# A projection of two gates in one pass, and a scan with its fillers in another order

## The chip, the cores and the metric

The kernel runs on one core of one Trainium2 chip. A core has TensorE (PE in the profile, with PEld for its weight loads), VectorE (DVE), ScalarE (ACT), GpSimd (POOL) and SyncE (SP, which issues nearly all DMAs here). The metric is device microseconds of one execution. Every engine works through its own list of instructions in order, and waits where the next one's inputs or its target buffer are not ready.

## The reference

One encoder layer over 1024 positions of width 1024, in float32: a normalized input goes through one projection whose columns feed four mixers, their outputs are joined, projected and added to the input; then a gated feed-forward layer follows. What matters here, cut short:

```python
proj = einsum('bsd,de->bse', rmsnorm(h), w_in)
y_a = pool_mixer(p_pool)                    # running means over 2, 4, 8, 16 positions, then a small product
y_b = p_u * mixed(layernorm(p_v))           # spatial gating: a 128x128 product along positions, gated by u
y_c = p_cb * causal_conv(p_cc * p_ch)       # short convolution, three projections of 256 columns
y_d = ssd(p_z, p_x, p_b, p_c, p_dt)         # a scan over chunks; its output is gated by silu(p_z), then normalized
h = h + concat(y_a, y_b, y_c, y_d) @ w_out
h = h + (silu(rmsnorm(h) @ w_gate) * (rmsnorm(h) @ w_up)) @ w_down
return rmsnorm(h)
```

## The kernel before

A program builds the lists of instructions; a scheduler inside it orders them by its own estimate of time, and an explicit `follow(i, j)` makes instruction i stand behind j on their engine. Nearly all large products are done in three passes (`mm3`, or the loop of `proj_T`): each operand is split into a high and a low part, and high x high, high x low and low x high are summed. An operand's split is a copy on ACT (the line of `nc.scalar.copy` in `split`) and a subtraction on DVE.

Two forms of projection come from the input x (`xh`, `xl`, eight tiles of 128 rows). `proj_T(i)` takes 128 columns of the weights and gives a result with channels on the partitions: 48 products with 512 columns each, into two banks of PSUM. `proj_N` gives 128 positions on the partitions: 24 products, here with 256 columns for z and 256 for u, into one bank. Weights for these are loaded raw into one of two buffers (`wraw`) and split into one of four pairs (`whi`, `wlo`).

The order of work: the projections of the scan's inputs (`proj_T` 0 to 5, of which 5 is the last), then z for eight blocks of 128 positions (`pn_z`, gated by ACT into `sz`, which lies in mix 4 and 5), then the scan. The scan is `ssd_block(b, prev)` for b = 0 to 7, in the profile the products `pt_x` (transposes of the inputs), `pg` (scores), `py` (the output; its second part takes the state `prev`) and `pst` (the new state). On DVE a block turns the scores into `Gm`, multiplies them into the decays `E`, and makes `xd`, `xe` and a first `y` out of `xb`, which ACT copies from `pt_x`; after `py` it adds up y and makes the next `prev`. All these small products take their PSUM from one pool of three banks (`pss`), in turn, and a bank is free again when what stands in it has been read. `ssd_end` normalizes finished blocks: a power on POOL, a scaling on DVE and the transposes `pty`.

Behind each block stands one part of the list `fill`: work that has nothing to do with the scan and keeps TensorE busy while DVE and ACT make the block's inputs. Before, that list is: the spatial gating of blocks 0 to 3 (with the four products `pm` and the projections `pn_u`), the gating of blocks 4 to 7, `pooling(0)`, `pooling(1)`, and `conv_c`, `conv_h` for t = 0, then for t = 1. `conv_h(t)` ends with two sums on DVE (the second and third tap) and then one multiplication of 128x1024 on POOL. `conv_b(0)` and `conv_b(1)` stand behind the whole scan in the code, but the scheduler put them between its last blocks. In names with numbers, pt10 is `conv_b(0)`, pt12 is `conv_h(1)` and pt13 is `conv_b(1)`.

Behind that stands the output projection (`po`), which takes the mixed tiles in the order of the list `order`, then the feed-forward layer, which is more than half of the time and which the change does not touch.

Of the kernel before, what the change touches and what calls it, by code (L numbers as in the profile page):

```python
# [46 lines left out]
def encoder_kernel(ctx, tc, xT, w_t, w_z, w_vd, w_u, pool_w, sgu_wT, par, row, w_out, w_gate, w_up, w_dp, w_dl, gfin, out):  # L47
# [94 lines left out]
    mix = [acts.tile([P, S], F32, name=f"mix{i}", tag="act") for i in range(8)]  # L142


    order = [2, 3, 0, 1, 6, 7, 4, 5]
    mh, ml = [None] * 8, [None] * 8
    h1 = [None] * 8

# [21 lines left out]
    with ExitStack() as a:  # L170
# [17 lines left out]
        def pc(c):  # L188
            return part[:, c:c + 1]
# [69 lines left out]
            o = (g % 2) * 64  # L259
            nc.sync.dma_start(out=pw[o:o + 64, g // 2, o:o + 64], in_=pool_w[g])  # L260

        def proj_T(*tiles, ws=None):

            ws = ws or [load_w(w_t[i], S, f"t{i}") for i in tiles]
            pss_ = [[psm.tile([P, HS], F32, name=f"pt{i}_{h}", tag="mm") for h in range(2)] for i in tiles]
            for k in range(NK):
                ks = slice(k * P, (k + 1) * P)
                for (hi, lo), ps in zip(ws, pss_):
                    for w1, x1, first, last in ((hi, xh, True, False), (hi, xl, False, False), (lo, xh, False, True)):
                        for h in range(2):  # L270
                            nc.tensor.matmul(ps[h], w1[:, ks], x1[k][:, h * HS:(h + 1) * HS],  # L271
                                             start=(k == 0 and first), stop=(k == NK - 1 and last))
            return pss_ if len(tiles) > 1 else pss_[0]

        def evac(ps, out):
# [124 lines left out]

        def heads(t):
            return t.rearrange("p (h c) -> p h c", h=NH)

        def ssd_block(b, prev):
            bs = slice(b * P, (b + 1) * P)
            E = sb.tile([P, NH, P], F32, name=f"E{b}", tag="E", bufs=2)
            nc.sync.dma_start(out=E, in_=acsD[b * NH:(b + 1) * NH, :].unsqueeze(0).to_broadcast([P, NH, P]))
            for h in range(NH):
                V.tensor_scalar(out=E[:, h, :], in0=E[:, h, :], scalar1=acs[:, b * NH + h:b * NH + h + 1],
                                scalar2=0.0, op0=ALU.subtract, op1=ALU.min)  # L410
            nc.scalar.activation(out=E, in_=E, func=AF.Exp)
# [12 lines left out]
            E4 = E.rearrange("p (g r) l -> p g r l", g=2)
            V.tensor_tensor(out=E4, in0=E4, in1=Gm.unsqueeze(2).to_broadcast([P, 2, 2, P]), op=ALU.mult)
            xd = sb.tile([P, 256], F32, name=f"xd{b}", tag="xd", bufs=1)
            xe = sb.tile([P, 256], F32, name=f"xe{b}", tag="xe", bufs=1)
            V.tensor_tensor(out=heads(xd), in0=heads(xb[:, 0:256]), in1=per_head(delta, b), op=ALU.mult)
            V.tensor_tensor(out=heads(xe), in0=heads(xb[:, 0:256]), in1=per_head(dte, b), op=ALU.mult)
            py = pss.tile([P, 512], F32, name=f"py{b}", tag="sm")  # L430
            for h in range(NH):
                nc.tensor.matmul(py[:, h * 64:(h + 1) * 64], E[:, h, :], xd[:, h * 64:(h + 1) * 64],
                                 start=True, stop=True)
            if prev is not None:
                for g in range(2):
                    nc.tensor.matmul(py[:, 256 + g * P:256 + (g + 1) * P], cT[g][:, bs],
                                     prev[:, g * P:(g + 1) * P], start=True, stop=True)
            y = yz[b]
            V.tensor_tensor(out=heads(y), in0=heads(xb[:, 0:256]),
                            in1=rowt[:, R_D:R_D + 4].unsqueeze(2).to_broadcast([P, NH, 64]), op=ALU.mult)  # L440
            V.tensor_tensor(out=y, in0=y, in1=py[:, 0:256], op=ALU.add)
            if prev is not None:
                yo = sb.tile([P, 256], F32, name=f"yo{b}", tag="yo", bufs=1)
                V.tensor_tensor(out=heads(yo), in0=heads(py[:, 256:512]), in1=per_head(ea, b), op=ALU.mult)
                V.tensor_tensor(out=y, in0=y, in1=yo, op=ALU.add)
            V.tensor_tensor(out=y, in0=y, in1=sz[b], op=ALU.mult)
            for g in range(2):
                jk = sb.tile([P, P], F32, name=f"jk{b}{g}", tag="jk", bufs=1)
                nc.scalar.activation(out=jk, in_=y[:, g * P:(g + 1) * P], func=AF.Square,
                                     accum_out=ss[:, 2 * b + g:2 * b + g + 1])  # L450
            if b < NB - 1:
                pst = pss.tile([P, 512], F32, name=f"pst{b}", tag="sm")
                for g in range(2):
                    nc.tensor.matmul(pst[:, g * P:(g + 1) * P], xb[:, 256 + g * P:256 + (g + 1) * P],
                                     xe[:, g * P:(g + 1) * P], start=True, stop=True)
                new = sb.tile([P, 256], F32, name=f"prev{b}", tag="prev", bufs=2)
                if prev is None:
                    V.tensor_copy(out=new, in_=pst[:, 0:256])
                else:
                    V.tensor_tensor(out=heads(new), in0=heads(prev), in1=per_head(dec, b), op=ALU.mult)  # L460
                    V.tensor_tensor(out=new, in0=new, in1=pst[:, 0:256], op=ALU.add)
                prev = new
            return prev

        def ssd_end(c0, n):
# [4 lines left out]
            for b0 in range(c0, c0 + n, 2):  # L470
# [13 lines left out]
        def mix_v():
            for h in range(NH):
                pm = pss.tile([P, 512], F32, name=f"pm{h}", tag="sm")
                v = vnt[:, :, h * 64:(h + 1) * 64]
                nc.tensor.matmul(pm, wTs[:, h, :], v, start=True, stop=True)
                nc.scalar.activation(out=v, in_=pm.rearrange("p (b c) -> p b c", b=NB), func=AF.Identity,
                                     bias=pc(C_SGUB + h))  # L490


        def gating(wu, b0):
            pt = pss.tile([P, 512], F32, name=f"ptb{b0}", tag="sm")
            for b in (b0, b0 + 1):
                ps = proj_N(wu, 256, b, "u")
                mb = vn[b]
                V.scalar_tensor_tensor(out=mb, in0=ps[:, :256], scalar=rn[:, b:b + 1], in1=mb,
                                       op0=ALU.mult, op1=ALU.mult)
                for g in range(2):  # L500
                    o = g * 256 + (b - b0) * P
                    nc.tensor.transpose(pt[:, o:o + P], mb[:, g * P:(g + 1) * P], ident)
            for g in range(2):
                nc.scalar.copy(out=mix[2 + g][:, b0 * P:(b0 + 2) * P], in_=pt[:, g * 256:(g + 1) * 256])


        def pooling(t):
# [40 lines left out]
            causal_conv(ch, 3, C_SCW + 3 * t, cc)  # L548
            nc.gpsimd.tensor_tensor(out=cc, in0=cc, in1=rB, op=ALU.mult)

        def conv_b(t):
            ps = proj_T(10 + 3 * t)
            for h in range(2):
                hs = slice(h * HS, (h + 1) * HS)
                V.tensor_tensor(out=mix[4 + t][:, hs], in0=ps[h], in1=gate_c[t][:, hs], op=ALU.mult)

        wu = nat_weights(w_u, 256, "u")
        fill = [lambda: (mix_v(), gating(wu, 0), gating(wu, 2)), lambda: (gating(wu, 4), gating(wu, 6)),
                lambda: pooling(0), lambda: pooling(1), lambda: conv_c(0), lambda: conv_h(0),
                lambda: conv_c(1), lambda: conv_h(1)]  # L560
        prev = None
        for b in range(NB):
            prev = ssd_block(b, prev)
# [519 lines left out]
```

## Time and profile before

| | us |
|---|---|
| three runs, median (lowest, highest) | 1011.45 (1010.33, 1013.96) |
| the profiled execution | 1012.61 |
| its span, first to last instruction | 1010.9 |
| PE busy | 999.5 (99%) |
| DVE busy | 814.4 (81%) |
| ACT busy | 402.4 (40%) |
| POOL busy | 297.8 (29%) |

The profiled execution is 1.7 us longer than its span, and 1.16 us above the median. A product's record on PE begins when it is issued, and lasts until its last result is out; the next is issued long before that. So the time that a product costs TensorE is the distance from its start to the start of the next one, not its own length. A plain float32 product takes two passes of this kind, so one instruction can have two records.

### The profile page before, as it was taken

To read this page: it belongs to the slowest core of one execution; us is meant where nothing else is said; L and a number is where in the kernel's file an instruction comes from. 1 tells how busy PE (TensorE), PEld (TensorE's weight loads), DVE (VectorE), ACT (ScalarE), POOL (GpSimd) and SP (SyncE) were. 2 spreads that over 40 slices of the span, in tenths; PEclk is the share of its full clock that TensorE was granted. 3 is DMA by queue.
4 is the path that set the end of the run, shared out by engine and by line. 5 is a ranking of instruction groups with operands and counts; after the bars stand their busy time and mean duration, and the time that the engine had idled before them with its cause. 6 is when DMAs were issued, how large, how long until landed. Compare 5 with 4: busy or idle time off the path is not lost.

```text
span 1010.9 us, 13188 instructions
## 1 busy us (share of the span) xinstructions
PE 999.5 (99%) x4816; PEld 840.1 (83%) x4816; DVE 814.4 (81%) x1293; ACT 402.4 (40%) x736; POOL 297.8 (29%) x329
## 2 busy tenths in 40 slices
PE   9999999999999999999999999999999999999996
PEld 8988998888887878888888888888888888888885
DVE  7498336786742689989899989989898999989867
ACT  8156322132531245434343343434343343334363
POOL 0034000011011131245434434544434434444302
PEclk9999999999999999999999999999999999999999
DMA  7311112101630201122111112111111111122204
GB/s 276 105 63 64 44 42 74 52 32 54 211 101 11 74 11 42 53 63 62 59 46 63 44 53 59 57 62 63 53 46 59 53 53 53 63 63 63 64 1 167
DMA packets 29681, 67.60 MB, mean 67 GB/s; under 512 B 3720, under 2 KB 4016, under 8 KB 29616
## 3 DMA queue, kind: packets, MB, share of 16 engines
q1 hardware_dynamic: 29184, 66.44, 19.9%
q8 instruction: 38, 0.62, 0.3%
q10 hardware_dynamic: 432, 0.31, 0.1%
q14 instruction: 27, 0.22, 0.1%
HBM read 62.53 MB, written 4.21 MB: 66 GB/s over the span
## 4 chain that ended last, share of the span: by engine, by line
PE 99%; DVE 1%; issue 0%; ACT 0%; POOLq 0%; POOL 0%; ACTq 0%
PE pt L271 15%; PE po L85 3%; PE po L87 3%; PE po L86 3%; PE p L85 1%; PE p L86 1%; PE p L87 1%; PE pn_v L86 1%; PE pn_z L87 1%; PE pn_z L86 1%; PE pn_z L85 1%; PE pn_u L86 1%; PE pn_v L87 1%; PE pn_u L85 1%; PE pn_u L87 1%; PE pn_v L85 1%
## 5 line engine op out<-in xcount | busy, mean ns | idle before, releaser
L815 POOL TENSOR_TENSOR rs<-rd 128x128 f32<-128x128 f32 x40 | 25.6, 641 | 187.3 <-DMA rd<-in_w_dp 80.5
L271 PE MATMUL pt<-x_lo,wh_t 128*128 128x512 f32 x224 | 70.3, 393 | 0.0
L271 PE MATMUL pt<-x_hi,wh_t 128*128 128x512 f32 x224 | 70.1, 394 | 0.0
L271 PE MATMUL pt<-x_hi,wl_t 128*128 128x512 f32 x224 | 69.6, 391 | 0.0
L940 ACT ACTIVATE g<-g 128x512 f32<-128x512 f32 x40 | 25.3, 633 | 71.1 <-DVE g L744 71.1
L92 ACT CAST dh<-rs 128x256 fp32r<-128x256 f32 (+1 forms) x80 | 28.1, 351 | 57.9 <-POOL rs L713 2.0
L93 DVE TENSOR_TENSOR dl<-rs,dh 128x256 fp32r<-128x256 f32 (+1 forms) x80 | 48.2, 603 | 1.5 <-ACT dh L92 1.5
L271 PEld LDWEIGHTS pt<-x_hi,wl_t 128*128 128x128 f32 x224 | 42.0, 188 | 8.7
L271 PEld LDWEIGHTS pt<-x_lo,wh_t 128*128 128x128 f32 x224 | 41.8, 188 | 8.5 <-issue 0.2
L271 PEld LDWEIGHTS pt<-x_hi,wh_t 128*128 128x128 f32 x224 | 41.7, 188 | 8.5 <-issue 0.2
L944 POOL TENSOR_TENSOR g<-g,u 128x512 f32<-128x512 f32 x20 | 34.1, 1703 | 36.4 <-DVE u L744 36.4
L85 PE MATMUL po<-mix_hi,oh 128*128 128x512 f32 x112 | 44.5, 398 | 0.0
L93 DVE TENSOR_TENSOR dl<-rd,dh 128x256 fp32r<-128x256 f32 x80 | 42.9, 537 | 1.8 <-ACT dh L92 1.8
L87 PE MATMUL po<-mix_hi,ol 128*128 128x512 f32 x112 | 44.2, 395 | 0.0
L86 PE MATMUL po<-mix_lo,oh 128*128 128x512 f32 x112 | 44.1, 394 | 0.0
L92 ACT CAST dh<-rd 128x256 fp32r<-128x256 f32 x80 | 32.2, 406 | 23.7 <-PE pd92A L86 1.6
L166 DVE TENSOR_TENSOR h<-po,h 128x512 f32<-128x512 f32 x16 | 11.0, 688 | 33.3 <-PE po L87 33.3
L752 POOL TENSOR_TENSOR s1u<-ru,ru 128x512 f32<-128x512 f32 x10 | 18.2, 1817 | 62.8 <-DMA ru<-in_w_up 51.3
L93 DVE TENSOR_TENSOR wl_t<-wr_t,wh_t 128x1024 fp32r<-128x1024 f32 (+2 forms) x16 | 17.4, 1087 | 22.0 <-ACT wh_t L92 22.0
L752 POOL TENSOR_TENSOR s1g<-rg,rg 128x512 f32<-128x512 f32 x10 | 12.9, 1293 | 59.9 <-DVE wg_2l L93 27.6
L612 POOL TENSOR_TENSOR qa_h<-qa_h,q 128x512 f32<-128x512 f32 x6 | 8.3, 1375 | 65.5 <-ACT q L611 65.5
L713 POOL TENSOR_TENSOR rd<-rd 128x128 f32<-128x128 f32 x40 | 26.6, 666 | 0.0
(3153 smaller groups left out, 3393.2 us busy)
## 6 DMA issues: line engine op xcount, KB each, us to landing
rd<-in_w_dp SPq DMA_DIRECT2D x40, 256.0 KB, 2.6
rg<-in_w_gate SPq DMA_DIRECT2D x40, 256.0 KB, 2.7
ru<-in_w_up SPq DMA_DIRECT2D x40, 256.0 KB, 2.8
wr_t<-in_w_t SPq DMA_DIRECT2D x12, 512.0 KB, 3.3
or<-in_w_out SPq DMA_DIRECT2D x8, 512.0 KB, 4.1
h<-in_xT SPq DMA_DIRECT2D x8, 512.0 KB, 5.0
mix<-in_xT SPq DMA_DIRECT2D x7, 512.0 KB, 7.7
out<-hn SPq DMA_DIRECT2D x7, 512.0 KB, 2.6
```

Of the source, the lines that this page charges most:

```text
L85: nc.tensor.matmul(ps, whi, xhi, start=start, stop=False, skip_group_check=skip)
L86: nc.tensor.matmul(ps, whi, xlo, start=False, stop=False, skip_group_check=skip)
L87: nc.tensor.matmul(ps, wlo, xhi, start=False, stop=stop, skip_group_check=skip)
L92: a = nc.scalar.copy(out=hi, in_=src)
L93: b = (eng or V).tensor_tensor(out=lo, in0=src, in1=hi.bitcast(F32), op=ALU.subtract)
L166: return V.tensor_tensor(out=h1[d][:, hs], in0=ps, in1=h1[d][:, hs], op=ALU.add)
L271: nc.tensor.matmul(ps[h], w1[:, ks], x1[k][:, h * HS:(h + 1) * HS], start=(k == 0 and first), stop=(k == NK - 1 and last))
L713: eng.tensor_tensor(out=out, in0=a_, in1=b_, op=ALU.subtract)
L752: G.tensor_tensor(out=s1, in0=a21, in1=a22, op=ALU.add)
L815: G.tensor_tensor(out=s1, in0=a21, in1=a22, op=ALU.add)
L940: nc.scalar.activation(out=t, in_=t, func=AF.Silu)
L944: (V if i in (1, 2) else nc.gpsimd).tensor_tensor(out=g[i], in0=g[i], in1=t, op=ALU.mult)
```

## The change

z and u are projected together: the 256 columns of either stand side by side in a tile of weights (four tiles of two rows of x each, filled by eight DMAs in place of four), so a block has 24 products with 512 columns, whose result is read by ACT (z) and by DVE (u, gated in place). The four products `pm` now stand ahead of this. The first filler, `gated`, only transposes the gated blocks. The list of fillers is now `gated`, `pooling(0)`, `pooling(1)`, `conv_c(0)`, `conv_c(1)`, `conv_h(0)`, `conv_h(1)`, `conv_b(0)`; and `conv_b(1)` stands behind the scan, its first product ordered behind the last product of the last `py`. In `order`, mix 4 comes earlier, since `conv_b(0)` now ends earlier.

```diff
-    order = [2, 3, 0, 1, 6, 7, 4, 5]
+    order = [2, 3, 0, 1, 4, 6, 7, 5]
...
-        wz = nat_weights(w_z, 256, "z")
+        for h in range(NH):
+            pm = pss.tile([P, 512], F32, name=f"pm{h}", tag="sm")
+            v = vnt[:, :, h * 64:(h + 1) * 64]
+            nc.tensor.matmul(pm, wTs[:, h, :], v, start=True, stop=True)
...
+        wzu = []
+        for j in range(4):
+            raw, hi, lo = w_tiles(S, f"zu{j}")
+            for i, w in enumerate((w_z, w_u)):
+                nc.sync.dma_start(out=raw.rearrange("p (k c) -> p k c", k=2)[:, :, i * 256:(i + 1) * 256],
+                                  in_=w[:, 2 * j:2 * j + 2, :])
+            split(raw, hi, lo)
+            wzu.append((hi, lo))
...
         for b in range(NB):
-            ps = proj_N(wz, 256, b, "z")
-            nc.scalar.activation(out=sz[b], in_=ps[:, :256], func=AF.Silu, scale=rn[:, b:b + 1])
+            ps = psm.tile([P, HS], F32, name=f"pn_zu{b}", tag="mm")
+            bs = slice(b * P, (b + 1) * P)
+            for k in range(NK):
+                hi, lo = (w_[:, k % 2 * HS:(k % 2 + 1) * HS] for w_ in wzu[k // 2])
+                mm3(ps, xh[k][:, bs], xl[k][:, bs], hi, lo, k == 0, k == NK - 1)
+            nc.scalar.activation(out=sz[b], in_=ps[:, 0:256], func=AF.Silu, scale=rn[:, b:b + 1])
+            V.scalar_tensor_tensor(out=vn[b], in0=ps[:, 256:512], scalar=rn[:, b:b + 1], in1=vn[b],
+                                   op0=ALU.mult, op1=ALU.mult)
...
-        def conv_b(t):
-            ps = proj_T(10 + 3 * t)
+        def conv_b(t, after=None):
+            ps = proj_T(10 + 3 * t, after=after)
...
-        wu = nat_weights(w_u, 256, "u")
-        fill = [lambda: (mix_v(), gating(wu, 0), gating(wu, 2)), lambda: (gating(wu, 4), gating(wu, 6)),
-                lambda: pooling(0), lambda: pooling(1), lambda: conv_c(0), lambda: conv_h(0),
-                lambda: conv_c(1), lambda: conv_h(1)]
+        fill = [gated, lambda: pooling(0), lambda: pooling(1), lambda: conv_c(0), lambda: conv_c(1),
+                lambda: conv_h(0), lambda: conv_h(1), lambda: conv_b(0)]
...
-        conv_b(0)
-        conv_b(1)
+        conv_b(1, last_py[-1])
```

How the lists of instructions look is shown at three places. TensorE, where the last scan input (pt5) ends and the projection of z begins. Before:

```order
L271 MATMUL pt5_0_887<-x_hi7_157,wl_t5_883 128x512
L271 MATMUL pt5_1_888<-x_hi7_157,wl_t5_883 128x512
L85 MATMUL pn_z0_984<-wh_z0_973,x_hi0_143 128x256
L86 MATMUL pn_z0_984<-wl_z0_974,x_hi0_143 128x256
L87 MATMUL pn_z0_984<-wh_z0_973,x_lo0_144 128x256
```

And now:

```order
L271 MATMUL pt5_0_887<-x_hi7_157,wl_t5_883 128x512
L271 MATMUL pt5_1_888<-x_hi7_157,wl_t5_883 128x512
L394 MATMUL pm0_972<-vnt_132,wTs_233 128x512
L394 MATMUL pm1_975<-vnt_132,wTs_233 128x512
L394 MATMUL pm2_978<-vnt_132,wTs_233 128x512
L85 MATMUL pn_zu0_1012<-wh_zu0_985,x_hi0_143 128x512
L86 MATMUL pn_zu0_1012<-wl_zu0_986,x_hi0_143 128x512
L87 MATMUL pn_zu0_1012<-wh_zu0_985,x_lo0_144 128x512
```

Three of the four `pm` came forward from the scan (the fourth stands inside the first block of z and u), and a pair of products with 256 columns became one with 512. TensorE at the last block of the scan, from the end of `conv_b(0)` (pt10) on. Before (29 products of pt13 stand between `pg7` and `py7`; "..." leaves out 27 of them):

```order
L271 MATMUL pt13_0_2338<-x_lo0_144,wh_t13_2333 128x512
L414 MATMUL pt_x7_2161<-ident_70,mix6_86 128x128
...
L420 MATMUL pg7_2168<-xbc4_879,xbc2_745 128x128
L420 MATMUL pg7_2168<-xbc5_946,xbc3_812 128x128
L271 MATMUL pt13_1_2339<-x_lo0_144,wh_t13_2333 128x512
...
L271 MATMUL pt13_1_2339<-x_hi5_153,wh_t13_2333 128x512
L432 MATMUL py7_2178<-xd7_2174,E7_2154 128x64 x4
```

And now:

```order
L271 MATMUL pt10_1_2071<-x_hi7_157,wl_t10_2066 128x512
L458 MATMUL py6_1921<-xd6_1917,E6_1897 128x64 x4
L462 MATMUL py6_1921<-prev5_1829,xbc4_879 128x128
L462 MATMUL py6_1921<-prev5_1829,xbc5_946 128x128
L481 MATMUL pst6_1938<-xe6_1918,xb6_1909 128x128 x2
L505 MATMUL pty4_2012<-ident_70,yzt_133 128x128 x4
L440 MATMUL pt_x7_2030<-ident_70,mix6_86 128x128
...
L446 MATMUL pg7_2037<-xbc5_946,xbc3_812 128x128
L458 MATMUL py7_2047<-xd7_2043,E7_2023 128x64 x4
L462 MATMUL py7_2047<-prev6_1941,xbc4_879 128x128
L462 MATMUL py7_2047<-prev6_1941,xbc5_946 128x128
L271 MATMUL pt13_0_2142<-x_hi0_143,wh_t13_2137 128x512
```

Nothing stands between `pg7` and `py7` any more, and all of pt13 comes behind `py7`. DVE around the scores of block 6, with the two sums of `conv_h(1)` (SCALAR_TENSOR_TENSOR on cc1). Before, the block's last inputs came first, and the sums behind them:

```order
L422 TENSOR_TENSOR Gm6_2051<-pg6_2048,tri_134 128x256
L278 TENSOR_TENSOR ch1_2195<-pt12_0_2203,rB_131 128x512
L278 TENSOR_TENSOR ch1_2195<-pt12_1_2204,rB_131 128x512
L425 TENSOR_TENSOR E6_2034<-E6_2034,Gm6_2051 128x512
L93 TENSOR_TENSOR wl_o1_2458<-wr_o1_2456,wh_o1_2457 128x1024
L547 TENSOR_TENSOR ch1_2195<-ch1_2195,cc1_2081 128x1024
L283 SCALAR_TENSOR_TENSOR cc1_2081<-ch1_2195,part_110,cc1_2081 128x1024 x2
```

And now:

```order
L468 TENSOR_TENSOR yzt_133<-yzt_133,py5_1809 128x256
L471 TENSOR_TENSOR yo5_1818<-py5_1809,ea_658 128x256
L488 TENSOR_TENSOR prev5_1829<-prev5_1829,pst5_1826 128x256
L286 SCALAR_TENSOR_TENSOR cc1_1701<-ch1_1944,part_110,cc1_1701 128x1024
L454 TENSOR_TENSOR xd6_1917<-xb6_1909,delta_635 128x256
L455 TENSOR_TENSOR xe6_1918<-xb6_1909,dte_661 128x256
...
L435 TENSOR_SCALAR E7_2023<-E7_2023,acs_657 128x128 x4
L473 TENSOR_TENSOR yzt_133<-yzt_133,mix5_85 128x256
L448 TENSOR_TENSOR Gm6_1914<-pg6_1911,tri_134 128x256
L451 TENSOR_TENSOR E6_1897<-E6_1897,Gm6_1914 128x512
```

The chain of `conv_h(1)` now runs ahead of block 6's inputs; its second sum, which sets off the multiplication on POOL, stands just ahead of `xd6`.

## Rows read from the trace of the kernel before

**Rows 1.** The page's chain that ended last: shares of the span by engine
```profile
PE 99%; DVE 1%; issue 0%; ACT 0%; POOLq 0%; POOL 0%; ACTq 0%
```

**Rows 2.** Windows: stretch, length, busy time of each engine, PE clock, DMA
```profile
121.90:250.00 128.10, 128.10 (x740) 110.44 (x739) 85.11 (x171) 33.27 (x72) 7.70 (x6) 1.00 0.17 54
...
328.00:330.00 2.00, 2.00 (x7) 1.52 (x6) 2.00 (x5) 1.76 (x3) 0.00 (x0) 0.50 0.00 0
...
366.00:370.00 4.00, 2.74 (x10) 1.34 (x9) 3.14 (x6) 0.30 (x1) 1.68 (x4) 1.00 0.23 66
```

**Rows 3.** Timeline of ACT: reading of two blocks of z in turn: start, length, instruction
```profile
110.55 0.47 ACT L392 ACTIVATE mix<-pn_z,rs_y_x 128x256 f32<-128x256 f32 x1 [2.41 <-PE pn_z L87]
113.43 0.47 ACT L392 ACTIVATE mix<-pn_z,rs_y_x 128x256 f32<-128x256 f32 x1 [2.41 <-PE pn_z L87]
```

**Rows 4.** Timeline of PE in the output projection
```profile
315.62 0.39 PE L85 MATMUL po<-mix_hi,oh 128*128 128x512 f32 x1
...
317.44 0.39 PE L87 MATMUL po<-mix_hi,ol 128*128 128x512 f32 x1
```

**Rows 5.** Timeline of PE: blocks 6 and 7 of the scan
```profile
243.07 1.00 PE L432 MATMUL py<-xd,E 128*128 128x64 f32 x8
...
244.41 0.61 PE L454 MATMUL pst<-xe,xb 128*128 128x128 f32 x4
244.85 0.60 PE L478 MATMUL pty<-ident,yzt 128*128 128x128 f32 x4
...
250.34 0.27 PE L414 MATMUL pt_x<-ident,mix 128*128 128x128 f32 x1
...
250.77 0.61 PE L420 MATMUL pg<-xbc,xbc 128*128 128x128 f32 x4
...
257.82 1.00 PE L432 MATMUL py<-xd,E 128*128 128x64 f32 x8
```

**Rows 6.** Timeline of DVE, 230 to 253 us
```profile
230.65 0.42 DVE L444 TENSOR_TENSOR yo<-py,ea 128x256 f32<-128x256 f32 x1
...
231.31 0.42 DVE L445 TENSOR_TENSOR yzt<-yzt,yo 128x256 f32<-128x256 f32 x1
...
234.79 0.47 DVE L409 TENSOR_SCALAR E<-E,acs 128x128 f32<-128x128 f32 x2
...
237.59 1.28 DVE L278 TENSOR_TENSOR ch<-pt,rB 128x512 f32<-128x512 f32 x2
238.78 0.68 DVE L425 TENSOR_TENSOR E<-E,Gm 128x512 f32<-128x512 f32 x1
239.38 1.22 DVE L93 TENSOR_TENSOR wl_o<-wr_o,wh_o 128x1024 fp32r<-128x1024 f32 x1
...
243.01 2.60 DVE L283 SCALAR_TENSOR_TENSOR cc<-ch,part,cc 128x1024 f32<-128x1024 f32 x2 [1.28 <-ACT cc L281]
...
246.53 1.85 DVE L445 TENSOR_TENSOR yzt<-yzt,yo 128x256 f32<-128x256 f32 x1
...
251.42 0.42 DVE L422 TENSOR_TENSOR Gm<-pg,tri 128x256 f32<-128x256 f32 x1 [0.51 <-PE pg L420]
...
252.77 0.68 DVE L425 TENSOR_TENSOR E<-E,Gm 128x512 f32<-128x512 f32 x1
```

**Rows 7.** Timeline of POOL: the multiplication that ends conv_h(1)
```profile
245.69 2.40 POOL L549 TENSOR_TENSOR cc<-cc,rB 128x1024 f32<-128x1024 f32 x1 [9.27 <-DVE cc L283]
```

**Rows 8.** Timeline of ACT, 245 to 252 us
```profile
245.49 0.84 ACT L480 ACTIVATE mix<-pty,part 128x256 f32<-128x256 f32 x2 [2.51 <-PE pty L478]
...
250.97 0.59 ACT L417 COPY xb<-pt_x 128x512 f32<-128x512 f32 x1 [1.21 <-PE pt_x L415]
```

**Rows 9.** Timeline of PE where it waits in the second half of the output projection
```profile
325.59 1.12 PE L139 MATMUL ps_rows_h<-rx_h,ones 4*128 4x512 f32 x2 [1.26 <-DVE rx_h L132]
...
328.26 0.63 PE L85 MATMUL po<-mix_hi,oh 128*128 128x512 f32 x1
...
331.25 0.45 PE L86 MATMUL po<-mix_lo,oh 128*128 128x512 f32 x1
```

More of the change, by code (lines that the diff above doesn't have):

```diff
@@ L260, in encoder_kernel, with proj_T @@
             nc.sync.dma_start(out=pw[o:o + 64, g // 2, o:o + 64], in_=pool_w[g])
-        def proj_T(*tiles, ws=None):
+        def proj_T(*tiles, ws=None, after=None):
             ws = ws or [load_w(w_t[i], S, f"t{i}") for i in tiles]
@@ L270, in proj_T @@
                         for h in range(2):
-                            nc.tensor.matmul(ps[h], w1[:, ks], x1[k][:, h * HS:(h + 1) * HS],
-                                             start=(k == 0 and first), stop=(k == NK - 1 and last))
+                            i = nc.tensor.matmul(ps[h], w1[:, ks], x1[k][:, h * HS:(h + 1) * HS],
+                                                 start=(k == 0 and first), stop=(k == NK - 1 and last))
+                            if after is not None:
+                                follow(i, after)
+                                after = None
             return pss_ if len(tiles) > 1 else pss_[0]
@@ L385, in encoder_kernel @@
             nc.gpsimd.tensor_tensor(out=v, in0=v, in1=rowt[:, R_LB:R_LB + 256], op=ALU.add)
-        wz = nat_weights(w_z, 256, "z")
+        for h in range(NH):
+            pm = pss.tile([P, 512], F32, name=f"pm{h}", tag="sm")
+            v = vnt[:, :, h * 64:(h + 1) * 64]
+            nc.tensor.matmul(pm, wTs[:, h, :], v, start=True, stop=True)
+            nc.scalar.activation(out=v, in_=pm.rearrange("p (b c) -> p b c", b=NB), func=AF.Identity,
+                                 bias=pc(C_SGUB + h))
+        wzu = []
[6 more added lines that the diff above has]
+            wzu.append((hi, lo))
         sz = [mix[4 + b // 4][:, (b % 4) * 256:(b % 4 + 1) * 256] for b in range(NB)]
         for b in range(NB):
-            ps = proj_N(wz, 256, b, "z")
-            nc.scalar.activation(out=sz[b], in_=ps[:, :256], func=AF.Silu, scale=rn[:, b:b + 1])
+            ps = psm.tile([P, HS], F32, name=f"pn_zu{b}", tag="mm")
[6 more added lines that the diff above has]
+                                   op0=ALU.mult, op1=ALU.mult)
         ss = sb.tile([P, NB * 2], F32, name="ss")
@@ L402, in heads @@
             return t.rearrange("p (h c) -> p h c", h=NH)
+        last_py = []
         def ssd_block(b, prev):
@@ L435, in ssd_block @@
                 for g in range(2):
-                    nc.tensor.matmul(py[:, 256 + g * P:256 + (g + 1) * P], cT[g][:, bs],
-                                     prev[:, g * P:(g + 1) * P], start=True, stop=True)
+                    i = nc.tensor.matmul(py[:, 256 + g * P:256 + (g + 1) * P], cT[g][:, bs],
+                                         prev[:, g * P:(g + 1) * P], start=True, stop=True)
+                last_py.append(i)
             y = yz[b]
@@ L481, in ssd_end, with gated @@
                                   mul=pc(C_NG + g))
[L484 to L499, printed above, removed]
+        def gated():
+            for b0 in range(0, NB, 2):
+                pt = pss.tile([P, 512], F32, name=f"ptb{b0}", tag="sm")
+                for b in (b0, b0 + 1):
+                    for g in range(2):
+                        o = g * 256 + (b - b0) * P
+                        nc.tensor.transpose(pt[:, o:o + P], vn[b][:, g * P:(g + 1) * P], ident)
                 for g in range(2):
[L501 to L504, printed above, removed]
+                    nc.scalar.copy(out=mix[2 + g][:, b0 * P:(b0 + 2) * P], in_=pt[:, g * 256:(g + 1) * 256])
         def pooling(t):
```

## The prediction

> **What bounds the kernel.** The chain that ended last comes first: 99% of it is PE [rows 1]. Then the windows: the whole scan is one stretch in which PE is busy for 128.10 of 128.10 us, at a granted clock of 1.00, so 2.4 GHz [rows 2]. So nothing that DVE, ACT, POOL or a DMA does in the scan costs anything now. The change can gain only by giving PE less to do, and it loses wherever PE must wait. Third, the timelines give each step's price and, on the other engines, how much room each has before PE would wait. Last, the places where PE does wait already: in the output projection it stands for 1.26 us behind DVE [rows 9], and 2.4 us later the clock reads 0.50, which is 1.2 GHz [rows 2].
>
> **Term 1, the merged projection: −2.5 us.** ACT reads one finished block of z every 113.43 − 110.55 = 2.88 us, and PE does nothing else there [rows 3]: 24 products with 256 columns, 0.120 us each. A product with 512 columns takes (317.44 − 315.62) / 8 = 0.2275 us [rows 4]. Two narrow ones cost 0.240, so a merged pair saves 0.0125 us. There are 8 blocks of 24 such pairs (z and u had 192 products each): 192 × 0.0125 = 2.4 us; with the rounding of the rows 2.3 to 2.6, and I take 2.5. The four `pm` and the transposes of the gated blocks are moved, not added. The new weights' eight DMAs stand where four did, and their splits are as many columns as before; PE reaches them only after pt5, and no wait follows by my estimate. The new DVE reading of u costs what it cost in the scan, and frees it there.
>
> Saying it as a fixed cost: 256 columns at 2.4 GHz are 106.7 ns and 512 are 213.3, so each product leaves some 13 to 14 ns over [rows 3, 4]. The Trainium skill ("TensorE: Matmul & The Clock Gate", Back-to-back issue gap) gives a warm product N / 2.4 GHz plus some 2.5 ns. By that the merge would save 192 × 2.5 ns = 0.5 us and the sum below would be 2.0 us longer; the rows of this kernel say 13, in both widths, and I go by them.
>
> **Term 2, a wait before py6: +2.0 us.** In the old order E6 stood ahead of the sums of `conv_h(1)` on DVE; now the whole chain from pt12's bank to the second sum stands ahead of it (the third place of the change), with `conv_b(0)` alone, pt10, as PE's cover. I count both engines from the end of pt12.
>
> PE: 48 products of pt10 are 48 × 0.2275 = 10.92; among them py5 at 244.41 − 243.07 = 1.34, pst5 at 244.85 − 244.41 = 0.44, pt_x6 at 250.77 − 250.34 = 0.43, and pg6 about as long as pst [rows 5]. PE is ready for py6 at 13.6.
>
> DVE, if it begins at e: from reading the bank to the first sum takes 243.01 − 237.59 = 5.42, less 0.60 for the E that stood between (239.38 − 238.78): 4.82. The two sums take 2.60 together, and three small steps on py5 and pst5 stand between them; small steps follow each other at (231.31 − 230.65) / 2 = 0.33 us [rows 6]. So POOL can start its multiplication at e + 4.82 + 2.60 + 1.0 = e + 8.4. It takes 2.40 [rows 7], and here is the disputed step. In before, y += yo began 0.84 us after it, and was 1.85 us long where the same instruction elsewhere took 0.42: it ended at 248.38, just behind POOL's end at 248.09 [rows 6, 7]. The steps ahead of it that read PSUM kept their 0.42 and 0.41 [rows 6]. I read this as: a DVE operation with both operands in SBUF that starts during POOL's multiplication waits for its end. Now xd6 slips in ahead, and xe6, with both operands in SBUF, is held to about e + 11.1. Behind it stand y, y += yo, the next prev, four steps of E7 (0.40 for two [rows 6]), y × z, Gm6 and E6: 5 × 0.33 + 0.8 + 0.68 = 3.1. E6 is ready at e + 14.2.
>
> How late is e? The same count for `conv_h(0)`, one filler earlier: py4 comes 22 products (5.0) after the end of pt9 and lasts 1.34, y and yo of block 4 take DVE to about 7.1, the first sum, two small steps, E6's four and the second sum to 11.1, POOL to 13.5, the held step to 13.85, and Gm5, E5, xd5, xe5, y to 15.8. PE ends pt12 at 10.92 + 1.34 + 0.44 for pst4, 2 × 0.44 for two groups of transposes, 0.43 and 0.44: 14.45. So e is about 1.4, and the wait 14.2 + 1.4 − 13.6 = 2.0 us. Bounds: without any hold by POOL e is 0 and E6 comes at 8.4 + 2 × 0.33 + 3.1 = 12.2, no wait; with the later hold alone, 0.6; with both and a late DMA of decays, 2.6.
>
> **Term 3, a wait before py7: +3.0 us.** Before, 29 products of pt13, 6.6 us, stood between pg7 and py7, and hid DVE's work on the scores. Now nothing stands there. Count from the start of py6. py6 and pst6 end at 1.78, then comes pty4. pt_x7 needs the bank of py6, which yo6 reads last; DVE first reads pt10's two banks (1.28, as for pt12 [rows 6]) and scales four tiles for pty4 (0.8, as E7's four), so yo6 ends near 2.9. pt_x7 starts then, and pg7 ends at 2.9 + 0.43 + 0.44 = 3.75 [rows 5]. Then DVE: from the start of Gm to the end of E took 252.77 + 0.68 − 251.42 = 2.03 us [rows 6], with xd, xe and y between, and these five stand there in the same order now. Gm begins 0.2 after pg (251.42 against 250.77 + 0.44 [rows 5, 6]), so E is ready at 6.0. ACT's xb (0.59, behind 0.84 for two copies of pty [rows 8]) ends near 4.1, in time for xd. PE has 3.1 us of work in these 6.0 (1.34, three times 0.44, 0.43): it waits 2.9, I take 3.0 with the start of py7. The lower bound is DVE's five steps alone, 2.03 + 0.2 + 0.1 = 2.3, since nothing can be put between; the upper one 3.6, if pty4's scaling is late. Behind py7 stands pt13, which loses nothing else: pty6 waits behind 33 of its products, and the output projection takes mix 5 last, three products per tile and 24 per block, so that DVE has over 4 us for its two splits.
>
> **Term 4, the clock: +1.6 us.** After the first wait of 1.26 us PE ran seven products in 331.25 − 328.26 = 2.99 us, 0.427 each in place of 0.2275 [rows 9]: 1.4 us lost, and 1.6 with the edges of the stretch. The second wait, as long (2.74 busy of 4.00), was followed by none: 1.00 throughout [rows 2]. So a wait of 1.3 us brings a low stretch in one of two cases. The two new ones together idle PE for 5 us within some 10, so I take one such stretch, with none (0) and two (3.2) as bounds.
>
> **Edits at nothing.** The new order of `conv_c` and pooling: PE has the same products, and DVE, busy for 85.11 of the scan's 128.10 us [rows 2], keeps by the same count some 4 us ahead of PE in each earlier block. `order` with mix 4 earlier only follows conv_b(0). If this cover is gone, the price is that of a wait like term 2's.
>
> **Sum.** 1012.61 − 2.5 + 2.0 + 3.0 + 1.6 = 1016.7 for an execution like the profiled one; that one was 1.16 above the median, so the median comes at **1015.6**, 0.4% over 1011.45. From no change this measurement can tell about 0.3%, 3.0 us.
>
> **Rivals.**
> - All four terms as above, 0.53. Its own range is 1013.8 to 1016.8: terms 2 and 3 together go from 3.2 to 6.2 in place of 5.0.
> - *Not slower:* POOL's multiplication doesn't hold xe6 (or the DVE chain runs early enough), so E6 is ready before PE. Place: DVE, from xd6 to E6. For it: the hold is read from one row. Against it: 1.85 against 0.42 [rows 6]. Term 2 goes: 1013.6, within 0.3%. It decides as soon as py6 waits less than about 0.9 us, since 1014.5 is the limit. 0.20.
> - The clock stays at 2.4 GHz after the waits, as after the second old one [rows 2]: 1014.0. 0.10.
> - The change does only what the merge does, and the waits are hidden: 1011.45 − 2.5 = 1008.9; against it stands term 3's lower bound of 2.3. It is faster by over 0.3% if the merge, and DVE's freed time in the scan, give 0.6 more than the rows say. 0.08, half of it faster.
> - Two low stretches, or the decays of block 7 late: 1.6 more, 1017.2. 0.07.
> - The merge saves 0.5, not 2.5: 1017.6. Only the rows' 13 ns per product speak against it. The page named above would have it so. 0.02.
>
> Within 0.3% (1008.4 to 1014.5) lie the second and third rival, half of the fourth, and the low end of the first case, some 0.03: 0.37 together. 0.04 is left for faster, and 0.59 for slower. The range from 1011.6 to 1018.0 leaves out the hidden waits below, and above it two low stretches on top of late waits.
>
> **What will show it.** Blocks of z and u read by ACT every 5.46 us. PE idle ahead of py6 by some 2 us and ahead of py7 by 2.3 to 3 (in pieces, with pt_x7), both released by DVE's E. xe of block 6 some 2 us long beside a POOL multiplication. A granted clock of 0.50 in pt13 behind. Wrong if py6 follows pt10 at once, if the clock stays 1.00 in pt13, or if PE waits in an earlier block or at the start of the new projection for its weights.

## The result, and the profile after

Six executions of the changed kernel took 1016.84 to 1019.01 us, with a median of **1017.87**; six of the kernel before, on the same chips, had a median of 1012.49. The ratio is 1.0051 (95% interval 1.0038 to 1.0063): slower by 5.2 us (3.8 to 6.4). Forecast were 1015.6 against 1011.45, so 4.1 us more.

The profiled execution took 1016.84 us (span 1015.1), the shortest of the six. The chain of its page, where [rows 1] had 99% and 1%:

```profile
PE 96%; DVE 3%; ACT 0%; issue 0%; POOLq 0%; POOL 0%; ACTq 0%
```

PE's waits in the changed kernel, by line (total, how often, the longest):

```profile
PE py L458 <- DVE E L451: 3.8, 2, 2.2
PE ps_rows_h L139 <- DVE rx_h L132: 2.5, 2, 1.3
PE ps_ones L186 <- POOL ones L67: 1.2, 1, 1.2
PE pt_x L440 <- DVE yo L471: 0.4, 1, 0.4
```

The second and the third were there before. New are the first, twice py behind DVE's E, and the last, pt_x7 behind yo6. A wait is counted from the end of what PE last put out; what it costs is read from starts. PE's timeline of blocks 6 and 7, as [rows 5]:

```profile
243.74 0.71 PE L271 MATMUL pt<-x_hi,wh_t 128*128 128x512 f32 x2
...
246.97 1.10 PE L458 MATMUL py<-xd,E 128*128 128x64 f32 x8 [1.61 <-DVE E L451]
...
249.92 0.30 PE L440 MATMUL pt_x<-ident,mix 128*128 128x128 f32 x1 [0.42 <-DVE yo L471]
...
250.38 0.61 PE L446 MATMUL pg<-xbc,xbc 128*128 128x128 f32 x4
253.21 1.94 PE L458 MATMUL py<-xd,E 128*128 128x64 f32 x8 [2.21 <-DVE E L451]
...
255.76 1.20 PE L271 MATMUL pt<-x_hi,wh_t 128*128 128x512 f32 x2
...
259.98 0.63 PE L271 MATMUL pt<-x_hi,wl_t 128*128 128x512 f32 x2
```

The first of these rows begins the six products of pt10 that stand behind pg6. At 0.2275 us each they end at 245.10, and py6 starts 1.9 us later. From py6 to py7 are 253.21 − 246.97 = 6.24 us with 3.1 us of work: 3.1 us lost. The first part of py7 is 1.94 long where py6's is 1.10. From py7 to 259.98 PE did py7 (1.34) and ten products of pt13 (2.28), 3.6 us of work in 6.8: **3.1 us lost to the clock**, which the windows show (stretch, length, busy of PE, PEld, DVE, ACT, POOL, clock, DMA), as [rows 2]:

```profile
254.30:259.80 5.50, 5.50 (x18) 4.63 (x19) 2.22 (x6) 1.86 (x6) 0.71 (x1) 0.51 0.00 0
...
330.00:336.00 6.00, 4.74 (x20) 3.22 (x18) 4.08 (x7) 3.08 (x5) 1.26 (x1) 1.00 0.12 44
```

The second of these rows is the wait of [rows 9] in the output projection: still 1.26 us, but this time the clock stays at 1.00 behind it, and the 1.6 us of before are not lost. DVE up to E6 and E7, as [rows 6]:

```profile
230.14 0.42 DVE L448 TENSOR_TENSOR Gm<-pg,tri 128x256 f32<-128x256 f32 x1 [1.30 <-PE pg L446]
230.60 1.02 DVE L451 TENSOR_TENSOR E<-E,Gm 128x512 f32<-128x512 f32 x1
...
232.56 1.28 DVE L281 TENSOR_TENSOR ch<-pt,rB 128x512 f32<-128x512 f32 x2
...
239.57 1.28 DVE L286 SCALAR_TENSOR_TENSOR cc<-ch,part,cc 128x1024 f32<-128x1024 f32 x1
240.77 0.42 DVE L454 TENSOR_TENSOR xd<-xb,delta 128x256 f32<-128x256 f32 x1
241.10 2.62 DVE L455 TENSOR_TENSOR xe<-xb,dte 128x256 f32<-128x256 f32 x1
...
246.22 0.69 DVE L451 TENSOR_TENSOR E<-E,Gm 128x512 f32<-128x512 f32 x1
...
252.38 0.68 DVE L451 TENSOR_TENSOR E<-E,Gm 128x512 f32<-128x512 f32 x1
```

And POOL beside it, as [rows 7]:

```profile
228.25 2.83 POOL L564 TENSOR_TENSOR cc<-cc,rB 128x1024 f32<-128x1024 f32 x1 [11.18 <-DVE cc L286]
241.02 2.42 POOL L564 TENSOR_TENSOR cc<-cc,rB 128x1024 f32<-128x1024 f32 x1 [9.94 <-DVE cc L286]
```

The second row is the multiplication of conv_h(1). xd6, which starts ahead of POOL, takes 0.42; xe6, which starts 0.08 behind it, takes 2.62, and ends 0.28 after POOL's end. That is the hold that the prediction had read from one row of before. ACT reads a block of z and u each 5.44 us, as [rows 3] had it for z alone:

```profile
113.46 0.47 ACT L414 ACTIVATE mix<-pn_zu,rs_y_x 128x256 f32<-128x256 f32 x1 [4.98 <-PE pn_zu L87]
118.90 0.47 ACT L414 ACTIVATE mix<-pn_zu,rs_y_x 128x256 f32<-128x256 f32 x1 [4.96 <-PE pn_zu L87]
```

By spans the account closes: −2.5 (merge) + 1.9 + 3.1 (waits) + 3.1 (clock in the scan) − 1.6 (no low clock in the output projection) = +4.0, and 1015.1 − 1010.9 is +4.2.

### The profile page after: what moved, and what is told of

The parts are those of the page before. It is cut to its first block, busy times and chain, and to the rows that moved or that the text cites. A ratio compares the mean times of both kernels' runs of the same rounds, so it can differ in the third digit from the quotient of the medians.

```text
span 1015.1 us, 12807 instructions
## 1 busy us (share of the span) xinstructions
PE 999.4 (98%) x4624; PEld 831.6 (82%) x4624; DVE 812.5 (80%) x1293; ACT 402.7 (40%) x736; POOL 298.4 (29%) x329
## 4 chain that ended last, share of the span: by engine, by line
PE 96%; DVE 3%; ACT 0%; issue 0%; POOLq 0%; POOL 0%; ACTq 0%
PE pt L271 14%; PE po L85 3%; PE po L86 3%; PE po L87 3%; PE p L85 1%; PE pn_zu L85 1%; PE p L87 1%; PE pn_zu L86 1%; PE p L86 1%; PE pn_zu L87 1%; PE pn_v L86 1%; PE pn_v L87 1%; PE pn_v L85 1%; PE ph L974 1%; PE ps_ones L186 1%; PE pn L87 1%
## 5 line engine op out<-in xcount | busy, mean ns | idle before, releaser
L415 DVE SCALAR_TENSOR_TENSOR vnt<-pn_zu,rs_y_x,vnt 128x256 f32<-128x256 f32 x8 | 3.9, 485 | 33.6 <-ACT mix L414 33.6
```

## The experiments

The theory: merging saves 2.5 us; the scan loses more, since nothing is left to put ahead of py6 and py7, and the clock falls behind these waits. Rivals are named with each run. "Clock" in the table is what the runs' mean granted clock stands for: (1 − clock) times the span, averaged over the executions. It is read in steps of 0.001, a microsecond of a single run, it counts a low clock while PE waits too, and it holds the low clock at the very end of an execution, when PE has no more products: 1.4 to 2.2 us in the traces of these kernels (in before PE's last product starts at 1002.84, and from 1008 to 1010 the clock reads 0.50).

| kernel | median us (runs) | before, same chip | ratio (95% interval) | clock us |
|---|---|---|---|---|
| the change | 1017.87 (6) | 1012.49 | 1.0051 (1.0038 to 1.0063) | 6.3 |
| free_pt13 | 1010.94 (12) | 1012.83 | 0.9979 (0.9970 to 0.9988) | 3.7 |
| narrow_zu | 1020.25 (5) | 1012.83 | 1.0071 (1.0059 to 1.0083) | 6.3 |
| dummy_py7 | 1015.87 (12) | 1012.83 | 1.0031 (1.0019 to 1.0043) | 4.2 |
| no_mul1 | 1015.17 (11) | 1012.83 | 1.0017 (1.0007 to 1.0027) | 4.7 |
| narrow_zu2 | 1019.33 (5) | 1012.78 | 1.0063 (1.0051 to 1.0075) | 6.1 |
| pin_pg7 | 1014.37 (11) | 1012.78 | 1.0016 (1.0007 to 1.0025) | 4.6 |
| old_fill | 1018.48 (6) | 1012.78 | 1.0047 (1.0031 to 1.0064) | 7.1 |
| old_fill_free_pt13 | 1011.69 (11) | 1012.78 | 0.9991 (0.9982 to 1.0000) | 3.6 |
| double_mul1 | 1021.21 (6) | 1013.56 | 1.0084 (1.0067 to 1.0101) | 8.7 |
| dummy_both | 1016.40 (10) | 1013.56 | 1.0028 (1.0017 to 1.0039) | 3.3 |

The kernel before has 3.9 in the last column (29 runs).

**free_pt13** undoes the last part of the change.

```diff
-        conv_b(1, last_py[-1])
+        conv_b(1)
```

> The change without its last part: conv_b(1) (pt13) is not ordered behind py7, and the scheduler puts 19 of its products ahead of py6 and 21 ahead of the transposes pt_x7, with py7 itself behind the first 21 products of the output projection. Theory: the time lost lies in the waits ahead of py6 (1.9 us) and py7 (3.1 us) and the low clock behind them (3.1 us), all for want of products to put there; then 1017.9 - 8.1 = 1009.8 us (1009.0 to 1011.5), no wait at py6 and py7, a granted clock of 1.00 in the scan, and so faster than before by what the merge saves. Rival: the waits only move, since py7 and pty6 now come late for the output projection, which then waits for mix 5 to 7: 1012.5 us or more, with PE idle in the output projection by 2 us more than before.

Its waits of PE:

```profile
PE ps_rows_h L139 <- DVE rx_h L132: 2.5, 2, 1.3
PE ps_ones L186 <- POOL ones L67: 1.2, 1, 1.2
```

py6 and py7 wait for nothing, and the list is that of the kernel before. The theory holds: the order behind py7, with nothing else changed, costs 7 us, and the rival (a wait that moves into the output projection) is out. This is the version that beats both kernels, by 2.1 us (1.2 to 3.0) against before. Its median is 1.1 above the forecast; the profiled execution, at 1012.18, had low clock behind both waits of the output projection:

```profile
249.00:265.00 16.00, 16.00 (x91) 13.81 (x89) 12.63 (x26) 7.58 (x17) 0.00 (x0) 1.00 0.50 165
...
322.00:330.00 8.00, 6.74 (x21) 4.64 (x20) 5.98 (x10) 3.69 (x6) 1.26 (x1) 0.79 0.10 33
...
364.00:376.00 12.00, 10.74 (x38) 7.79 (x37) 11.15 (x19) 4.81 (x9) 4.36 (x7) 0.86 0.09 22
```

**narrow_zu** and **narrow_zu2** take the merge out of the change and leave all else. In narrow_zu the two halves of a bank are begun in turn, and z and u do not come out in full; narrow_zu2 sums up each half whole.

```diff
-                mm3(ps, xh[k][:, bs], xl[k][:, bs], hi, lo, k == 0, k == NK - 1)
+                for c in range(2):
+                    cs = slice(c * 256, (c + 1) * 256)
+                    mm3(ps[:, cs], xh[k][:, bs], xl[k][:, bs], hi[:, cs], lo[:, cs], k == 0, k == NK - 1, skip=True)
```

> The change with z and u side by side in the same tiles, but each pair multiplied by two products with 256 columns again (48 per block in place of 24); the rest stands as it was. Theory (13 ns over the columns' own time in each product, as the rows of before had it): 192 x 12.5 ns = 2.4 us longer than the change, 1020.3 us, and a block read every 5.76 us in place of 5.45. Rival (2.5 ns of fixed cost per product): 0.5 us longer, 1018.4 us, a block every 5.50 us. Second rival: the wide product costs as much as two narrow ones, no difference.

narrow_zu2 has the loop over c outside that over k.

> As narrow_zu, but each block has all 24 products of z with 256 columns and then all 24 of u, so that each half of the bank is summed up whole. Theory: 2.4 us over the change again, 1020.3 us, whatever the order of the narrow products. Rival: the 2.4 us of narrow_zu came from alternating the halves of the bank, and the sequence of the kernel before costs less: 1018.5 us.

In the trace of narrow_zu2, ACT reads a block every 5.76 us, in narrow_zu too:

```profile
113.56 0.47 ACT L416 ACTIVATE mix<-pn_zu,rs_y_x 128x256 f32<-128x256 f32 x1 [5.29 <-PE pn_zu L87]
...
119.32 0.47 ACT L416 ACTIVATE mix<-pn_zu,rs_y_x 128x256 f32<-128x256 f32 x1 [5.29 <-PE pn_zu L87]
```

(5.76 − 5.44) × 8 = 2.56 us, as the theory has it; 192 products at 2.5 ns would make 0.06 us per block. The medians lie 2.4 and 1.5 us over the change, by the ratios 2.0 and 1.2; with five runs each and an interval of 1.2 us to either side they fit the 2.5, but they alone would not rule out 0.5. The block time does.

**dummy_py7** fills the wait ahead of py7 with work for nothing (`last_pg` is the last product of pg7).

```diff
+            if b == 7:
+                for k in range(10):
+                    i = nc.tensor.matmul(py, xh[k % NK][:, bs], xh[k % NK][:, 0:HS], start=True, stop=True)
+                    follow(i, last_pg)
```

> The change with ten products of 512 columns that serve nothing put between pg7 and py7 (2.27 us of work in a wait of 2.3; their result is overwritten); the instructions on all engines up to py7 stand in the same order. Theory: py7 starts as late as before, 6.2 us behind py6, but PE isn't idle ahead of it, and the granted clock stays at 1.00 behind: 3.1 us less, 1014.8 us. Rival: the clock falls because of the idle time ahead of py6 or of the small products of the last blocks: then py7 and pt13 run at 0.50 as they do now, and the time stays at 1017.9 us.

PE's timeline, and the clock from py6 on:

```profile
246.76 1.10 PE L462 MATMUL py<-xd,E 128*128 128x64 f32 x8 [1.60 <-DVE E L451]
...
250.54 2.55 PE L459 MATMUL py<-x_hi 128*128 128x512 f32 x10
252.93 1.09 PE L462 MATMUL py<-xd,E 128*128 128x64 f32 x8
```

```profile
247.00:258.00 11.00, 10.58 (x66) 9.13 (x66) 8.62 (x23) 4.19 (x13) 0.99 (x1) 1.00 0.00 0
252.90:260.00 7.10, 7.10 (x38) 6.13 (x38) 4.94 (x11) 3.87 (x10) 0.52 (x1) 1.00 0.12 36
```

py7 starts 6.17 us behind py6 (6.24 in the change), so the time that DVE needs is the same; but py7 runs at full speed, and pt13 behind it at 1.00. The clock's loss is thus a loss of its own, brought by PE being idle. In the scan of this execution all of it is gone. In the median 2.0 us are saved, not 3.1, and the executions go from 1013.63 to 1019.10: those at 1018 and 1019 have a mean clock of 0.993 or 0.994, as the change has. So the rival seems to hold in a part of the executions: the wait ahead of py6 is still there, and pin_pg7 below shows that it can bring the low clock by itself.

**dummy_both** has seven more such products ahead of py6.

> As dummy_py7, with seven more products that serve nothing among the last of pt10, 1.6 us of work in the wait ahead of py6. pst6 and two DVE steps stand in a slightly other order here. Theory: E6 and E7 come as late as in the change, so the time that is not the clock's stays, but PE is idle for less than 1 us in all before py7 and the clock stays at 1.00 in every execution: 1015.4 us (1014.8 to 1016.2), with executions closer together than those of dummy_py7. Rival: the low clock doesn't hang on the idle time: as dummy_py7 or the change, 1016 to 1018 us, with a granted clock of 0.50 in pt13 in some.

Half a miss. The mean clock is the best of all (3.3 us), in line with the theory, but the time isn't better than dummy_py7's against before: other rows stand on DVE there, and pg7 now waits for yo6:

```profile
251.94 0.68 PE L446 MATMUL pg<-xbc,xbc 128*128 128x128 f32 x4 [1.38 <-DVE yo L475]
```

So PE was idle for more than the 1 us that the expectation had set, and behind this wait of 1.38 us, in this execution, the clock stayed at 1.00. It did not in every one, as had been expected: those of 1018.08 and 1018.20 us have a mean clock of 0.995. The executions do lie closer together than dummy_py7's (3.9 us from lowest to highest, against 5.5).

**no_mul1** leaves POOL's multiplication at the end of conv_h(1) out (that half of the channels lacks its scale).

```diff
-            nc.gpsimd.tensor_tensor(out=cc, in0=cc, in1=rB, op=ALU.mult)
+            if t == 0:
+                nc.gpsimd.tensor_tensor(out=cc, in0=cc, in1=rB, op=ALU.mult)
```

> The change without POOL's multiplication at the end of conv_h(1) (the second half of the convolution's channels is left without its scale); all other instructions stand in the same order. Theory: POOL's multiplication holds xe6 on DVE for 2.2 us and with it E6; without it xe6 takes 0.42 us, E6 comes 2.2 us earlier and py6 follows pt10 with a wait under 0.2 us: 1.9 us less, 1016.0 us, or down to 1014 if the clock's low stretch gets shorter too. Rival: the sums on DVE themselves make E6 late and xe6 would be late anyway: py6 still waits 1.2 us or more, 1017.3 us or above.

DVE's timeline, and PE's:

```profile
241.11 0.41 DVE L455 TENSOR_TENSOR xe<-xb,dte 128x256 f32<-128x256 f32 x1
...
244.49 0.69 DVE L451 TENSOR_TENSOR E<-E,Gm 128x512 f32<-128x512 f32 x1
```

```profile
245.24 1.11 PE L458 MATMUL py<-xd,E 128*128 128x64 f32 x8
```

xe6 starts at the same time as in the change (241.11, 241.10) and takes 0.41 in place of 2.62. E6 starts 1.73 us earlier (Gm6 now waits for pg6 a little), and py6 follows pt10 with under 0.2 us lost. The theory holds; by the medians 2.7 us were saved, by the ratios 3.4: 1.7 of the wait, and the rest of the clock. The wait ahead of py7 is still there, 2.21 us by the profile's count, and the windows behind it read:

```profile
252.00:255.00 3.00, 3.00 (x15) 2.54 (x15) 1.60 (x4) 0.20 (x1) 0.00 (x0) 0.65 0.00 0
255.00:258.00 3.00, 3.00 (x12) 2.43 (x11) 1.96 (x6) 2.31 (x8) 1.01 (x1) 0.78 0.00 0
```

That is 3.00 × 0.35 + 3.00 × 0.22 = 1.7 us of clock behind one wait, where the change lost 3.1 behind two.

**double_mul1** puts a second multiplication behind it, into a tile that nobody reads.

```diff
             nc.gpsimd.tensor_tensor(out=cc, in0=cc, in1=rB, op=ALU.mult)
+            if t == 1:
+                nc.gpsimd.tensor_tensor(out=ch[:, 2:2 + S], in0=cc, in1=rB, op=ALU.mult)
```

> The change with a second multiplication of the same size on POOL right behind that of conv_h(1); its result goes into a tile that nobody reads any more. DVE's and TensorE's instructions up to py6 stand in the same order. Theory: each multiplication holds the DVE step with two operands in SBUF that stands next, xe6 by the first, y or y += yo by the second, 2.4 us more in all: py6 waits 4.3 us, 1020.3 us (to 1021.5 with more low clock). Rival: after the first hold DVE runs freely and POOL shares or waits itself: py6 waits 1.9 to 2.4 us, 1018.4 us or less.

DVE, POOL and PE in turn:

```profile
241.36 0.42 DVE L454 TENSOR_TENSOR xd<-xb,delta 128x256 f32<-128x256 f32 x1
241.70 2.62 DVE L455 TENSOR_TENSOR xe<-xb,dte 128x256 f32<-128x256 f32 x1
244.24 2.59 DVE L466 TENSOR_TENSOR yzt<-xb,rowt 128x256 f32<-128x256 f32 x1
```

```profile
241.62 2.42 POOL L564 TENSOR_TENSOR cc<-cc,rB 128x1024 f32<-128x1024 f32 x1 [9.94 <-DVE cc L286]
244.11 2.44 POOL L566 TENSOR_TENSOR ch<-cc,rB 128x1024 f32<-128x1024 f32 x1
```

```profile
249.73 1.97 PE L458 MATMUL py<-xd,E 128*128 128x64 f32 x8 [3.78 <-DVE E L451]
```

Each of POOL's multiplications holds one step of DVE, 2.62 and 2.59 us long, and the wait of py6 grows from 1.61 to 3.78 by the profile's count, so by about one multiplication. By starts, counted as in the change, it loses 4.0 us, where 4.3 were expected; against before the kernel is 8.5 us slower, 3.3 more than the change, which is the multiplication and more low clock. DVE doesn't get its turn within one of them, only at its end. The Trainium skill says as much ("SBUF — State Buffer", SBUF: two separate sides): the port pair that DVE and GpSimd share is an exclusive lock, held for a whole instruction, and the other engine blocks. The rows here agree, with 2.42 us for the holder.

**pin_pg7** orders conv_b(1) behind pg7 in place of py7, so that 29 of its products come ahead of py7.

```diff
-        conv_b(1, last_py[-1])
+        conv_b(1, last_pg[-1])
```

> The change with conv_b(1) ordered behind pg7 in place of py7: 29 of its products stand between pg7 and py7, as in the kernel before; everything up to pg7 stands in the same order. Theory: py6 waits 1.9 us and pt_x7 0.4 as they do now, py7 not at all (2.4 us less), and with one wait in place of two the low clock comes in some of the executions only, 1 to 3 us less in the mean: 1013.5 us (1012.5 to 1015.0). Rival: the wait ahead of py6 alone brings the whole low stretch, or pty6, now late, makes the output projection wait: 1015.5 us or more.

PE's start of py6, and the windows behind it:

```profile
247.22 1.23 PE L459 MATMUL py<-xd,E 128*128 128x64 f32 x8 [1.61 <-DVE E L452]
```

```profile
247.20:248.90 1.70, 1.68 (x11) 1.69 (x12) 1.70 (x6) 0.00 (x0) 1.01 (x1) 0.75 0.02 5
248.90:251.00 2.10, 2.10 (x12) 2.10 (x11) 1.91 (x7) 0.00 (x0) 0.00 (x0) 0.50 0.00 0
```

py6 waits as in the change, py7 not at all, and 3.5 us are gone, within the expectation. Here the wait ahead of py6 alone brought a stretch at 0.50. In dummy_py7 the same wait, 1.60 us behind the same instructions, brought none.

**old_fill** gives the fillers their old order, **old_fill_free_pt13** frees pt13 too.

```diff
-        fill = [gated, lambda: pooling(0), lambda: pooling(1), lambda: conv_c(0), lambda: conv_c(1),
-                lambda: conv_h(0), lambda: conv_h(1), lambda: conv_b(0)]
+        fill = [gated, lambda: pooling(0), lambda: pooling(1), lambda: conv_c(0), lambda: conv_h(0),
+                lambda: conv_c(1), lambda: conv_h(1), lambda: conv_b(0)]
```

> The change with the list of fillers as it was before (conv_h(0) ahead of conv_c(1)); conv_b(1) stays behind py7. DVE's chain from pt12's bank to E6 stands in the same order, but POOL's multiplication of conv_h(0) now lies a filler earlier, so DVE reads pt12's bank at once and not some 0.95 us late. Theory: the delays add up, so py6 waits about 0.9 us in place of 1.9, and py7 3 us as now: 1016.9 us, or down to 1016 if the low clock gets rarer. Rival: the order of the fillers is without influence on block 6, since only the later multiplication counts: py6 waits 1.9 us, 1017.9 us.

A miss. POOL, DVE and PE of old_fill:

```profile
213.10 2.52 POOL L564 TENSOR_TENSOR cc<-cc,rB 128x1024 f32<-128x1024 f32 x1 [28.87 <-DVE cc L286]
```

```profile
230.93 0.42 DVE L448 TENSOR_TENSOR Gm<-pg,tri 128x256 f32<-128x256 f32 x1 [2.31 <-PE pg L446]
...
233.01 1.28 DVE L281 TENSOR_TENSOR ch<-pt,rB 128x512 f32<-128x512 f32 x2
```

```profile
247.43 1.19 PE L458 MATMUL py<-xd,E 128*128 128x64 f32 x8 [1.75 <-DVE E L451]
```

POOL's first multiplication is long over (213.10 + 2.52), and DVE still comes to pt12's bank late. What it waited for is pg5, as in the change ([1.30 <- PE pg] at 230.14 there, 2.31 here); Gm5, E5, xd5, xe5 and y stand ahead of the bank, and with 5 products (7 in the change) between pg5 and the end of pt12 they don't fit. py6 waits as long as ever. The rival of this run was right. But POOL has a part in the change: E5 there, begun at 230.60 while the multiplication of conv_h(0) runs (228.25 to 231.08), takes 1.02 in place of 0.68, so 0.34 us of DVE's 1.0 are a hold. old_fill has no such hold and two products fewer, and this run does not separate the two.

> The merged projection alone, as nearly as it can be had: fillers in the order of before, conv_b(1) not ordered behind py7 (both conv_b are placed by the scheduler, 21 products of pt13 ahead of py6). Theory: only the merge's gain is left, 1012.8 - 2.4 = 1010.4 us (1009.5 to 1011.5), as with free_pt13, whose order of fillers then is worth nothing by itself. Rival: the order of the fillers has a gain of its own, and this kernel is slower than free_pt13 by 1 us or more.

Between the two: above the range of the theory, and slower than free_pt13 by 0.75 us in the medians and 1.2 in the ratios, whose intervals overlap. The gain against before is 0.9 us (0.0 to 1.8), less than the merge's 2.5. Its profile has three waits that free_pt13's lacks:

```profile
PE pt L271 <- ACT wh_t L92: 0.5, 1, 0.5
PE pty L505 <- DVE yzt L503: 0.5, 1, 0.5
PE pt L271 <- ACT x_hi L96: 0.3, 1, 0.3
```

Together they make 1.3 us, as much as its span of 1011.8 exceeds free_pt13's 1010.5. The two of pt lie at 9 and 10 us, long before the fillers, and pin_pg7's and dummy_both's traces have the first of them too. Only the other bears on the fillers: pty6 stands in the output projection there and comes 0.5 us before its input. Whether the order of the fillers is worth more than that, and what else is missing against 2.5, can't be told from the spread of the runs.

## Why the prediction was right, and where a term was off

It was right in sign and in the place and size of each wait. The median of 1017.87 is within the range, but 0.1 below its upper end, and outside the 1013.8 to 1016.8 of the case that was held most likely. What came is nearest to the rival with two low stretches (1017.2), which had been given 0.07.

- **Merge, −2.5 us: right.** 5.44 us a block against 5.76 gives 2.56. In whole kernels it shows less surely: free_pt13 gains 2.1 us on before (1.2 to 3.0), old_fill_free_pt13 0.9 (0.0 to 1.8). The rival that would have made it 0.5 is out.
- **Wait ahead of py6, 2.0 us: measured 1.9.** The chain ran as laid out: from reading the bank at 232.56 to the end of E6 at 246.91 are 14.35 us, where the prediction counted 14.2. xe6 was held; without POOL's multiplication the wait is gone (no_mul1), with two it is a multiplication longer (double_mul1). The rival on the other side, no hold, is out. One step was wrong in its cause: DVE's late start at pt12's bank (e) was put down to the multiplication of conv_h(0). It is 1.0 us, not 1.4, and 0.34 of it is a hold by POOL (E5); the rest is that pg5 stands only a few products ahead of the end of pt12, and old_fill, without that hold but with pg5 two products nearer to it, is as late. That the wait still came out near the forecast is in part luck.
- **Wait ahead of py7, 3.0 us: measured 3.1**, with pt_x7 at 2.95 behind py6 (forecast 2.9) and E7 ready at 6.1 (6.0). pin_pg7 takes it away.
- **The clock, +1.6 us: too small.** The profiled execution lost 3.1 us behind py7, the top of the range given. In the mean over the runs the change loses 6.3 − 3.9 = 2.4 us more to the clock than before. The price of a stretch taken from [rows 9] holds for one wait: 1.7 in no_mul1. The step that failed is the count, one such stretch for the two new waits together: behind both, the time at 0.50 cost twice that, and it lay over py7 too.

With that, −2.5 + 1.9 + 3.1 + 2.4 = +4.9 against the 5.2 measured. The forecast median was off by 2.3 us, of which 1.0 is that before has a median of 1012.5 with more runs, not 1011.45, and 0.8 the clock (2.4 in place of 1.6).

## What to carry to other kernels

Work that hides another engine's chain is worth what it hides at the place where it stands: an order that puts all 48 products of one projection behind py7 cost 7 us, nearly three times what merging two projections had saved. Before ordering independent work behind a chain, look for the last place where that chain leaves TensorE with nothing, and leave some of the work free there. A GpSimd operation set off just ahead of short DVE steps that read no PSUM made the first of them as long as itself here (2.62 us beside 2.42); count it as part of DVE's chain.

## What the runs showed of the hardware

- The spread of the runs goes with the clock. Of the 29 executions of the kernel before in the first series, which go from 1010.59 to 1014.63, five have a mean clock of 0.998 and take 1011.15 us in the mean, thirteen have 0.996 or 0.997 and take 1012.65, and eleven have 0.995 and take 1014.26. The steps of 1.5 and 1.6 us are about what one stretch at 0.50 cost in [rows 9].
- The hold between POOL and DVE is not only for steps with two tiles in SBUF, and it works both ways. In before, four TENSOR_SCALAR steps on E took 3.01 us from 218.18 on, beside POOL's multiplication of conv_h(0) (218.00, 2.51 long); in the change the four of E7 take 0.86. And in the change, y × z of block 4, begun at 228.42, 0.17 us behind the start of POOL's first row, took its usual 0.42, while POOL took 2.83 in place of 2.42.
- The same wait behind the same instructions is followed by 0.50 in one execution and by 1.00 in another: 1.6 us ahead of py6 in pin_pg7 and dummy_py7, and 1.26 us in the output projection before and after the change. What decides it, no run here tells.
